# A two-layer diffusion backbone on one core: openings in a fixed order, modulation sums behind them, three direct chunks and another order of transfers in the first sub-layer, norms by chunk

## The chip, the cores and the metric

The kernel runs on one core of a Trainium2 chip. The metric is the device time of one execution in microseconds (us): the time before is the median of three runs. A profile is one further execution, recorded instruction by instruction; its own time is given beside its span (first to last instruction).

## The reference, cut to what matters

Two layers of three sub-layers each, over 512 latent tokens (`x`) and 256 context tokens (`ctx`) of width 1024. All numbers are float32.

```python
def norm_modulate(x, g, shift, scale):
    return rms_norm(x, g) * (1 + scale) + shift

def swiglu(h, w_in, w_out):
    gate, up = jnp.split(h @ w_in, 2, axis=-1)
    return (jax.nn.silu(gate) * up) @ w_out
...
for i in range(DEPTH):                       # DEPTH = 2
    m_lat = (silu(c) @ ada_w[i] + ada_b[i])  # 9 vectors of 1024: shift, scale, gate of 3 sub-layers
    m_ctx = (silu(c_ctx) @ ada_w[i] + ada_b[i])
    x = x + 0.5 * gate * swiglu(norm_modulate(x, ...), ffn_w_in[i, 0], ffn_w_out[i, 0])     # d_ff = 2816
    x = x + gate * mixer(norm_modulate(x, ...))   # layer 0: short gated conv; layer 1: attention, 8 heads, 2 kv heads
    x = x + 0.5 * gate * swiglu(norm_modulate(x, ...), ffn_w_in[i, 1], ffn_w_out[i, 1])
return rms_norm(x_lat, final_g)
```

Every sub-layer runs on both token groups with their own modulation (`m_lat`, `m_ctx`), but for the last one, which runs on the latent tokens alone.

## The kernel before, in words

**Layout and precision.** The stream `x` stays on the chip as eight tiles (m = 0 to 7) of 128 features by 768 tokens. Tokens are cut in two ways: into the two halves of 384 (`TOKENS`, `one` and `two`), or into 512 latent and 256 context tokens (`BOTH`). Each operand of a matmul is split in a rounded part and a rest (`split`: ScalarE copies to the high part, L178, VectorE subtracts for the low part, L179), and each product is three matmuls (`mm3`, L737 to L739).

**Weights.** They come as 512 KB transfers into a ring of five raw buffers (`raw_fill`, L197, SP's queue), are split into eight granules `w` (`w_fill`), and used in the order of one list. The splits of the last `out` of a sub-layer may go into "held" slots that the inputs no longer need.

**A sub-layer (FFN or conv).** Its columns are cut in chunks of two units of 128 columns (gate and up). A chunk is done either *directly*: two token halves times two halves of the features, which is 4 x 4 x 2 x 3 = 96 matmuls of 384 tokens; or by seven *products* of a Strassen-like scheme (M1 to M7; 7 x 4 x 3 = 84 matmuls). A direct step `(c, "01")` is chunk c, token half 0, feature half 1. The products need sums of the inputs (T1 to T4) and their splits, which direct chunks need not, so the first chunks of a sub-layer are direct (`FFN_DIRECT` = 2, `CONV_DIRECT` = 3) while VectorE makes the sums. Part by part of the columns, an `out` phase multiplies by the second weights and adds into `x` (L804, or L861 in the last phase, `out_close`).

**Between sub-layers: the opening.** `out_close` makes a first pass over token half one and a second over half two. Behind each of its matmul groups stand pieces of the next norm: `squares` (L543, L546, L547), `parts` (L566, L567), `root` (the matmul that sums over features, L573 and L574, then the reciprocal root, L555 to L559), `normed` (x times the root, L676), `modulated` (L684) and `parted` (the split into tiles B11, B21 for half one, B12, B22 for half two; 11 and 21 are the two feature halves). The rest stands in hooks behind quarters of the direct steps (`OPENING`): hook `(n, k)` runs after quarter k of step n, hook `n` after step n. Ahead of attention and of the last sub-layer, `out_steps` and `norm_mod` do the same with whole 128-feature chunks and 512, 256 or 128 tokens.

**Modulation.** The first six half-vectors are made by small matmuls during the boot (`ada_direct`, L437 to L445). The other 30 are made in the background by VectorE: `ada_task` has eight steps of sums (`acc`, L454 and L456, one or two per 256 KB transfer `aw`, which POOL issues, L465, two buffers), then `cut` into three bf16 pieces (L486, L488) and `fin`, twelve small matmuls (L494). `bg` runs one step per product from the second chunk behind the direct ones on, and `bg_end` what is left.

**Who sets the order.** TensorE and SP run in the order of the program throughout. ScalarE and VectorE run in the order of a planner, which works from estimated times, but for stretches that are written to keep the program's order (`in_order` to `free_order`): the instructions made in such a stretch keep their order among themselves, and others may be put between them. `keep_in_program_order` ties a single instruction into that order.

Of the kernel before, what the change touches and what calls it, by code (L numbers as in the profile page):

```python
# [36 lines left out]
FFN_DIRECT, CONV_DIRECT = 2, 3  # L37
# [27 lines left out]
HELD_AFTER_T = ((6, 7), (10, 11))  # L65
# [13 lines left out]
def product_order(count, parts, direct, boot=False):  # L79
# [15 lines left out]
    if boot:  # L95
        order += [(0, "00"), (1, "00"), (0, "01"), (1, "01")]
    else:
        order += [(0, "00"), (0, "01"), (1, "00"), (1, "01")]
    for c in range(2):
        order += [(c, "10"), (c, "11")]  # L100
        done(c)
    for c in range(2, direct):
        order += [(c, "10"), (c, "00"), (c, "11"), (c, "01")]
        done(c)
    order += [(direct, m) for m in ("M1", "M2", "M5", "M6")]
# [12 lines left out]
def backbone(ctx: ExitStack, tc: tile.TileContext, a: dict, out: bass.AP):  # L118
# [73 lines left out]
    def raw_fill(most=RAWS):  # L192
        while raw_state["open"] < most and raw_state["loaded"] < len(raws):
            n = raw_state["loaded"]
            src, (u, k), users = raws[n]
            t = wp.tile([P, D], F32, name=f"raw{n}", tag="raw", bufs=RAWS)[:, : u * k * P]
            nc.sync.dma_start(t.rearrange("p (u k c) -> p u k c", u=u, c=P) if len(src.shape) == 4 else t.rearrange("p (k c) -> p k c", c=P), src)  # L197
            raw_tiles[n] = [t.rearrange("p (u k c) -> p u k c", u=u, c=P), users]
            raw_state["loaded"] += 1
            raw_state["open"] += 1  # L200

    def raw_used(n):
        raw_tiles[n][1] -= 1
        if not raw_tiles[n][1]:
            raw_tiles.pop(n)
            raw_state["open"] -= 1

    traced = set()
    held_tiles = {}
    ready = []  # L210
    state = {"next": 0, "open": 0, "extra": 0, "used": 0}

    def place(n, where, k):
# [3 lines left out]
        elif where[0] == "slot":  # L217
            t = slot(where[1], [2, D // 2], f"w{n}")
        else:
# [62 lines left out]
    def add_out(w, k0, npart, held=None, key="", events=(None, None), extra=None, event=None):  # L282
        for m in range(0, KC, 2):
            n = raw_add(w[:, m : m + 2, k0 : k0 + npart, :], (2, npart), 2)
            for u in range(2):
                mm = m + u
                if held and mm < 6:
# [5 lines left out]
    def add_products(key, sources, order, parts, direct, out_w, held):  # L293
# [10 lines left out]
        for c, m in order:  # L304
            if m == "out":
                last = c == len(parts) - 1
                outs = out_w(c)
                add_out(*outs, held=held if last else None, key=f"{key}held", events=((key, "M5"), (key, "M6")))
                continue
            for which in range(2):  # L310
                need(c, which)
            if c >= direct:
                add_product(raw[c, 0], raw[c, 1], m)
            elif (c, m[1]) not in seen:
                seen.add((c, m[1]))
                k0 = 4 * int(m[1])
                for which in range(2):
                    add_plain(raw[c, which], 0, slice(k0, k0 + 4))
# [32 lines left out]
    ffn_order = {boot: product_order(FC, FFN_PARTS, FFN_DIRECT, boot) for boot in (False, True)}  # L351
# [10 lines left out]

    def w_list():
        f0 = starts(LAST_PARTS)

        def ffn_products(i, s):
            b = 2 * i + s // 2
            sources = [[a["ffn_w_in"][b, f][:, z] for z in range(2)] for f in range(FC)]
            f0 = starts(FFN_PARTS)
            add_products(f"f{i}{s}", sources, ffn_order[(i, s) == (0, 0)], FFN_PARTS, FFN_DIRECT, lambda p: (a["ffn_w_out"][b], f0[p], FFN_PARTS[p]), HELD_AFTER_T)  # L370

        ffn_products(0, 0)
# [51 lines left out]
    def ada_load(i, hm, tiles):  # L424
        loaded = []
        for k in range(KC):
            w = tiles[k // 3][:, k % 3, :]
            nc.sync.dma_start(w, a["ada_w"][i, hm, :, k, :])
            loaded.append(w)
        return loaded  # L430

    def ada_direct(i, hm, loaded, tag):

        ps = ptile(tag)
        for k in range(KC):
            g = 32 * (k % 4)
            pe.matmul(ps[g : g + 32, :], boot_tiles["silu"][:, k, :], loaded[k], start=(k < 4), stop=(k >= 4), tile_position=(0, g), skip_group_check=True)  # L437
# [5 lines left out]
        pt = ptile("S", (P, 4, P))  # L443
# [8 lines left out]
    def ada_add(acc, w, k, v, first):  # L452
        if first:
            dve.tensor_scalar_mul(acc, w, silu_c[:, k, v : v + 1])  # L454
        else:
            dve.scalar_tensor_tensor(out=acc, in0=w, scalar=silu_c[:, k, v : v + 1], in1=acc, op0=ALU.mult, op1=ALU.add)  # L456
# [3 lines left out]
    def ada_next(n):  # L460

        if n < len(ada_chunks):
            i, hm, k = ada_chunks[n]
            w = ada_loaded[n] = apool.tile([P, 512], F32, name=f"aw{i}_{hm}_{k}", tag="aw", bufs=2)
            nc.gpsimd.dma_start(w, a["ada_w"][i, hm, :, k, :])  # L465

    def ada_task(i, hm, nv):
# [5 lines left out]
        def step(k):  # L473
# [3 lines left out]
            for v in range(nv):  # L477
                ada_add(st["acc"][:, v, :], w, k, v, k == 0)
# [11 lines left out]
        def fin(v):  # L490
# [5 lines left out]
            if v == nv - 1:  # L496
                ada_done.add((i, hm))
                task_done[0] += 1

        steps = [lambda k=k: step(k) for k in range(KC - 1)]  # L500
        steps.append(lambda: (step(KC - 1), cut(0)))
        if nv == 2:
            steps.append(lambda: (fin(0), cut(1)))
# [1129 lines left out]
```

## Time and profile before

| | |
|---|---|
| median of 3 runs | 2640.86 us (2633.59 to 2642.06) |
| the profiled execution | 2634.72 us, span 2633.0 us, mean granted clock 0.972 |
| TensorE (PE) busy | 2488.1 us, 94% |
| VectorE (DVE) busy | 1960.9 us, 74% |
| ScalarE (ACT) busy | 1169.4 us, 44% |
| moved from HBM | 244.97 MB |

In rows by instruction, a row gives the start, the duration, the engine, the line, `out<-in`, the shapes, and in brackets the idle time of the engine before it with what ended it. Rows of waits give the sum, the count and the longest. A matmul's duration is longer than its distance to the next, since matmuls are pipelined: the distance is what counts. The granted clock is the share of TensorE's full clock that was given.

### The profile page before, as it was taken

What the parts mean: (1) busy time and instruction counts of PE and PEld (TensorE: products, weight loads), DVE (VectorE), ACT (ScalarE), POOL (GpSimd) and SP (SyncE); (2) the same over time, 40 slices, a digit from 0 to 9 for tenths busy, and PEclk for the clock granted to TensorE, in tenths of its full rate; (3) what the DMA queues carried; (4) which work ended last, traced back from release to release, by engine and by line L of the source; (5) the groups of instructions that cost most, each with busy time, mean ns of one, the idle gap of its engine ahead of it and who ended that gap; (6) DMA issues with size and microseconds to landing.
All of it is one profiled execution on the core that took longest, in us unless ns stands there. A gap on an engine that the chain in (4) does not pass through costs nothing.

```text
span 2633.0 us, 36845 instructions
## 1 busy us (share of the span) xinstructions
PE 2488.1 (94%) x14180; PEld 2292.0 (87%) x14180; DVE 1960.9 (74%) x3511; ACT 1169.4 (44%) x2161; POOL 130.9 (5%) x248
## 2 busy tenths in 40 slices
PE   6899999998999899999999899999998999999997
PEld 3799899997989789998999798899997789888886
DVE  5899897568998799888866886766676887644444
ACT  5454353345434544534535453443344785432232
POOL 0010110000000001011000111100000000000000
PEclk9899999998999899999999899999999999999999
DMA  8142342121223123333311243411230201222220
GB/s 321 61 148 96 127 136 74 64 97 59 96 92 95 45 94 125 119 113 129 112 57 60 96 142 111 136 65 65 67 126 33 73 1 53 90 98 96 96 88 33
DMA packets 92193, 249.46 MB, mean 95 GB/s; under 512 B 10224, under 2 KB 19568, under 8 KB 92016
## 3 DMA queue, kind: packets, MB, share of 16 engines
q1 hardware_dynamic: 72816, 184.18, 20.7%
q0 software_dynamic: 19200, 62.93, 7.1%
q8 instruction: 111, 1.82, 0.3%
q14 instruction: 66, 0.54, 0.1%
HBM read 244.97 MB, written 2.10 MB: 94 GB/s over the span
## 4 chain that ended last, share of the span: by engine, by line
PE 59%; issue 21%; DVE 10%; DMA 6%; ACT 3%; POOL 0%; DVEq 0%; POOLq 0%; ACTq 0%
PE ps_A L738 12%; PE ps_A L737 12%; PE ps_A L739 12%; DMA aw<-in_ada_w 6%; PE ps_C L737 5%; PE ps_C L738 5%; PE ps_C L739 5%; DVE acc L456 2%; PE ps_B L737 2%; PE ps_B L738 2%; PE ps_B L739 2%; DVE w L179 1%; PE ps_T L1365 1%; ACT f L684 1%; ACT w L178 0%
## 5 line engine op out<-in xcount | busy, mean ns | idle before, releaser
L178 ACT ACTIVATE w<-raw 128x512 fp32r<-128x512 f32 (+2 forms) x819 | 502.1, 619 | 740.7 <-PE ps_A L739 419.5
L179 DVE TENSOR_TENSOR w<-raw,w 128x512 fp32r<-128x512 f32 (+2 forms) x819 | 550.3, 678 | 194.3 <-ACT w L178 185.6
L456 DVE SCALAR_TENSOR_TENSOR acc<-aw,silu_c,acc 128x512 f32<-128x512 f32 x364 | 266.6, 747 | 59.5 <-DMA aw<-in_ada_w 58.8
L737 PE MATMUL ps_A<-gh,w 128*128 128x512 f32 (+2 forms) x648 | 221.2, 341 | 3.7 <-ACT w L178 3.6
L739 PE MATMUL ps_A<-gh,w 128*128 128x512 f32 (+2 forms) x648 | 221.1, 341 | 1.7 <-DVE w L179 1.7
L738 PE MATMUL ps_A<-gl,w 128*128 128x512 f32 (+2 forms) x648 | 221.2, 341 | 0.5 <-DVE gl L179 0.5
L465 POOL DMA_DIRECT2D aw<-in_ada_w x240 | 129.7, 540 | 1564.3 <-DVE acc L454 895.6
L737 PE MATMUL ps_C<-gh,w 128*128 128x512 f32 (+2 forms) x496 | 177.8, 358 | 19.3 <-DVE g L989 14.0
L804 DVE SCALAR_TENSOR_TENSOR x<-ps_A,gat,x 128x512 f32<-128x512 f32 (+1 forms) x200 | 122.4, 615 | 88.4 <-PE ps_A L739 87.9
L739 PE MATMUL ps_C<-gh,w 128*128 128x512 f32 (+2 forms) x496 | 176.2, 355 | 3.3 <-DVE w L179 3.3
L738 PE MATMUL ps_C<-gl,w 128*128 128x512 f32 (+2 forms) x496 | 177.4, 358 | 0.5 <-DVE gl L179 0.2
L737 PE MATMUL ps_A<-h,w 128*128 128x512 f32 (+1 forms) x424 | 165.3, 390 | 9.3 <-ACT sq L546 9.3
L738 PE MATMUL ps_A<-hl,w 128*128 128x512 f32 (+1 forms) x424 | 165.0, 389 | 0.0
L739 PE MATMUL ps_A<-h,w 128*128 128x512 f32 (+1 forms) x424 | 164.9, 389 | 0.0
L325 DVE TENSOR_TENSOR raw<-raw,raw 128x512 f32<-128x512 f32 x207 | 142.2, 688 | 5.4 <-DMA raw<-in_ffn_w_in 2.8
L737 PEld LDWEIGHTS ps_A<-gh,w 128*128 128x128 f32 x648 | 124.2, 192 | 20.0 <-ACT w L178 4.4
L738 PEld LDWEIGHTS ps_A<-gl,w 128*128 128x128 f32 x648 | 124.0, 191 | 16.2 <-DVE gl L179 1.9
L739 PEld LDWEIGHTS ps_A<-gh,w 128*128 128x128 f32 x648 | 124.1, 192 | 15.5 <-DVE w L179 2.6
L804 DVE SCALAR_TENSOR_TENSOR x<-ps_C,gat,x 128x512 f32<-128x512 f32 (+1 forms) x136 | 87.8, 646 | 54.6 <-PE ps_C L739 54.5
L486 ACT ACTIVATE pc<-acc 128x512 bf16<-128x512 f32 x156 | 95.9, 625 | 71.5 <-DVE acc L488 40.0
L737 PEld LDWEIGHTS ps_C<-gh,w 128*128 128x128 f32 x496 | 95.7, 193 | 34.6 <-issue 15.1
L739 PEld LDWEIGHTS ps_C<-gh,w 128*128 128x128 f32 x496 | 95.7, 193 | 17.0 <-DVE w L179 5.1
(379 smaller groups left out, 6574.7 us busy)
## 6 DMA issues: line engine op xcount, KB each, us to landing
raw<-in_ffn_w_in SPq DMA_DIRECT2D x176, 512.0 KB, 3.7
aw<-in_ada_w POOLq DMA_DIRECT2D x240, 256.0 KB, 3.0
raw<-in_ffn_w_out SPq DMA_DIRECT2D x76, 512.0 KB, 3.9
raw<-in_conv_w_in SPq DMA_DIRECT2D x24, 512.0 KB, 4.1
ada<-in_ada_w SPq DMA_DIRECT2D x37, 256.0 KB, 5.4
raw<-in_attn_w_qkv SPq DMA_DIRECT2D x12, 512.0 KB, 5.2
raw<-in_conv_w_out SPq DMA_DIRECT2D x8, 512.0 KB, 3.6
raw<-in_attn_w_o SPq DMA_DIRECT2D x8, 512.0 KB, 3.6
```

Of the source, the lines that this page charges most:

```text
L178: act.activation(dsth, src, AF.Copy)
L179: dve.tensor_tensor(out=dstl, in0=src, in1=dsth.bitcast(F32), op=ALU.subtract)
L325: dve.tensor_tensor(out=quad(o), in0=quad(x), in1=quad(y), op=ALU.subtract)
L456: dve.scalar_tensor_tensor(out=acc, in0=w, scalar=silu_c[:, k, v : v + 1], in1=acc, op0=ALU.mult, op1=ALU.add)
L465: nc.gpsimd.dma_start(w, a["ada_w"][i, hm, :, k, :])
L486: act.activation(pc, acc, AF.Copy)
L684: act.activation(at, at, AF.Identity, scale=scl[:, m, v : v + 1], bias=mods[i][:, 3 * s, m, v : v + 1])
L737: pe.matmul(ps, wh, xh, start=first, stop=False, **kw)
L738: pe.matmul(ps, wh, xl, start=False, stop=False, **kw)
L739: pe.matmul(ps, wl, xh, start=False, stop=last, **kw)
L804: dve.scalar_tensor_tensor(out=x, in0=p[:, o - off : o - off + w], scalar=gat[:, m, v : v + 1], in1=x, op0=ALU.mult, op1=ALU.add)
L1365: pe.transpose(pt[:, c, :], pr[:, (c0 + c) * P : (c0 + c + 1) * P], ident)
```

## The change

In words:

1. First sub-layer: three direct chunks instead of two, all first token halves ahead of all second ones. The first two weights come as half transfers with the rest behind the shift's weights; the gates' modulation weights go through the ring of raw buffers, the first two background transfers onto SP's queue behind the last direct step. Some splits go to other homes in memory.
2. All openings: the squares, norms and splits stand in a new order, all in program order on ScalarE and VectorE; `modulated` may put every second chunk, or its short pieces, on VectorE. Evictions of direct steps are held and run at a later hook; the fourth pair of banks is B and S.
3. The first two products of the first chunk behind the direct ones (M1, M2) stand ahead of the first `out` phase. A third pair of held slots.
4. Background: the first sum of each sub-layer is tied to the program order, the steps are spread evenly from the eighth product to the last but two chunks, and an empty step (`rest`) stands between `cut` and `fin`.
5. Ahead of attention and of the last sub-layer, the norm is cut in steps of one chunk, put behind groups of the second pass (`PASS_STEPS`); the root of the second group stands later; the last sub-layer opens with three chunks of its first half instead of two.

The diff, cut to its core:

```diff
-FFN_DIRECT, CONV_DIRECT = 2, 3
+FFN_DIRECT, CONV_DIRECT, BOOT_DIRECT = 2, 3, 3
-HELD_AFTER_T = ((6, 7), (10, 11))
+HELD_AFTER_T = ((6, 7), (10, 11), (8, 9))
...
     if boot:
-        order += [(0, "00"), (1, "00"), (0, "01"), (1, "01")]
+        order += [(c, "0" + k) for k in "01" for c in range(direct)]
+        order += [(c, "1" + k) for c in range(direct) for k in "01"]
...
-    order += [(direct, m) for m in ("M1", "M2", "M5", "M6")]
+    order += [(direct, m) for m in ("M1", "M2")]
+    for c in range(direct):
+        done(c)
+    order += [(direct, m) for m in ("M5", "M6")]
...
+            if split:
+                nc.sync.dma_start(dst[:, :, : k // 2], src[:, :, : k // 2])
+                raw_late.append((dst[:, :, k // 2 :], src[:, :, k // 2 :]))
...
+            for hm in (4, 5):
+                boot_raws[hm] = [raw_add(a["ada_w"][0, hm, :, k : k + 2, :].rearrange("p k (j c) -> p k j c", c=P), (2, 4), 2) for k in range(0, KC, 2)]
...
+                ins = ada_add(st["acc"][:, v, :], w, k, v, k == 0)
+                if pinned[0]:
+                    tc.keep_in_program_order(ins)
+            pinned[0] = False
...
         steps.append(lambda: (step(KC - 1), cut(0)))
+        steps.append(rest)
...
+        pace["n"] += 1
+        if pace["n"] < pace["first"]:
+            return
+        span = pace["last"] - pace["first"] + 1
+        due = min(pace["steps"], -(-pace["steps"] * (pace["n"] - pace["first"] + 1) // span))
+        while pace["done"] < due:
+            ada_tasks.pop(0)[1]()
+            pace["done"] += 1
...
-            with tc.manual_schedule(engines=CHAIN_ORDERED):
-                parts = norm_parts(passes[0])
-                run(passes[1], *held[0], False)
-                if width == 2:
-                    run(passes[1], *held[1], False)
-                for step in after(passes[0], parts):
-                    step()
-                for m in range(held[4 - width][0][0]):
-                    sq_add(m, passes[1])
+            in_order()
+            steps = iter(after(passes[0], norm_parts(passes[0])))
+    PASS_STEPS = {1: {0: [("squares", (0,))], 1: [("squares", (1,))], 2: [("norm", 1)], 3: [], 4: [("squares", (2,)), ("norm", 1)], 5: [("norm", 1)], 6: [],
+                      7: [("norm", 7), ("squares", range(3, 8))]},
...
-        behind = {1: [("root", 0)], 2: [("whole", 0, 0, 0)], 3: [("whole", 0, 0, 1), ("parted", 0, 0, 0)], 4: [("whole", 1, 0, 0), ("parted", 0, 0, 1)],
-                  5: [("whole", 1, 0, 1), ("parted", 1, 0, 0)], 6: [("parted", 1, 0, 1), ("squares", 1, range(2))], 7: [("squares", 1, range(2, 6))]}
+        behind = {0: [("squares", 1, [0])], 1: [("root", 0), ("squares", 1, [1]), ("normed", 0, 0, 0)], 2: [("modulated", 0, 0, 0), ("normed", 0, 0, 1), ("parted", 0, 0, 0, "hi"), ("squares", 1, [2])],
...
-    OPENING = {(0, 0): [("squares", 1, range(6, 8)), ("parts", 1)], (1, 1): [("root", 1)], (1, 3): [("whole", 0, 1, 0), ("whole", 0, 1, 1)],
+    OPENING = {(0, 0): [("squares", 1, [7])], (0, 2): [("parts", 1)], (2, 0): [("root", 1)],
+               (2, 1): [("normed", 0, 1, 0), ("modulated", 0, 1, 0, "short"), ("parted", 0, 1, 0, "hi"), ("normed", 0, 1, 1)],
...
+               (3, 1): [("parted", 1, 1, 1, "lo")], (4, 1): [("evict",)], (4, 2): [("sums", "T1", 0)], (4, 3): [("sums", "T1", 1)], (5, 0): [("sum_parted", "T1", 0)],
...
-                if k == 2:
+                if k == 2 and half:
                     w_fill(1)
...
-            scale0 = ada_direct(0, 2, ada_load(0, 2, ada_slots(6, 7, 8)), "C")
-            raw_fill(2)
-            shift0 = ada_direct(0, 0, ada_load(0, 0, ada_slots(9, 10, 11)), "C")
+            scale0 = ada_direct(0, 2, ada_load(0, 2, ada_slots(6, 7, 8)), "C", "A")
+            raw_fill(2, True)
+            shift0 = ada_direct(0, 0, ada_load(0, 0, ada_slots(9, 10, 11)), "C", "A")
+            raw_rest()
+            raw_fill(4)
...
-            gate0 = ada_direct(0, 4, ada_load(0, 4, ada_gs(0, 2) + ada_slots(6)), "B")
-            gate1 = ada_direct(0, 5, ada_load(0, 5, ada_slots(7, 8, 9)), "A")
+            gate0 = ada_direct(0, 4, ada_raws(4), "B")
+            gate1 = ada_direct(0, 5, ada_raws(5), "B")
...
+                     (2, 3): do(("squares", 1, range(4))), (3, 0): do(("squares", 1, range(4, 6)), ("fill", 2)), (3, 1): do(("squares", 1, range(6, 8))), (3, 2): do(("parts", 1), ("fill", 2)),
+                     (4, 0): do(("gate0", 3)), (4, 1): do(("root", 1)), (4, 2): do(("normed", 0, 1, 0), ("modulated", 0, 1, 0, "short"), ("parted", 0, 1, 0, "hi"), ("normed", 0, 1, 1)),
...
+                     (8, 2): do(("gate1", 1)), (8, 3): do(("gate1", 2)), (9, 0): do(("gate0", 1)), (9, 1): do(("gate1", 1)), (10, 1): do(("sums", "T3", 0), ("sums", "T3", 1)),
+                     11: do(("sum_parted", "T1", 0), ("sum_parted", "T1", 1), ("sums", "T2", 0), ("sums", "T2", 1), ("more",)),
...
-            for c in range(2):
-                ps = banks(other, 2)
+            for c in range(3):
+                ps = banks(other, 2)
...
             k_project(lat, 0)
+            q_project(0, 0)
             settle()
-            q_project(0, 0)
```

More of the change, by code (lines that the diff above doesn't have):

```diff
@@ L919, in gated, with products @@
         return got
[L921 removed]
+    behind_outs = []
+    def products(gp, key, order, parts, direct, chunk, straight, out_args, after, passes, hooks, hold):
         live = {}
```

328 lines of the change are left out of this document (189 added, 139 removed).

## The prediction

> **What bounds the kernel now.** I read the page first (shares of the engines), then the stretches of the span, then TensorE's waits, then the order of time where the waits are long.
>
> ```profile
> span 2633.0 us, 36845 instructions
> ...
> PE 2488.1 (94%) x14180; PEld 2292.0 (87%) x14180; DVE 1960.9 (74%) x3511; ACT 1169.4 (44%) x2161; POOL 130.9 (5%) x248
> ```
>
> TensorE (PE) is the bound, and only 145 us of its span are idle. So a change of order alone can win those 145 us and what a slow clock costs beside them, and nothing more. The stretches say where they lie (length, then busy time of each engine, granted clock near the end):
>
> ```profile
> 28.60:60.50 31.90, 28.30 (x170) 20.90 (x170) 18.91 (x36) 15.83 (x29) 1.08 (x2) 0.95 0.93 335
> 60.50:105.50 45.00, 27.60 (x127) 24.96 (x124) 37.89 (x62) 27.19 (x52) 3.24 (x6) 0.75 0.21 71
> 105.50:585.00 479.50, 471.59 (x2839) 451.18 (x2838) 392.16 (x675) 209.36 (x383) 34.51 (x64) 0.99 0.31 105
> 585.00:660.00 75.00, 64.33 (x335) 61.58 (x334) 61.22 (x108) 37.66 (x67) 4.31 (x8) 0.91 0.17 57
> 868.00:940.00 72.00, 55.20 (x254) 48.49 (x253) 58.38 (x92) 40.43 (x75) 4.31 (x8) 0.86 0.19 64
> 940.00:1430.00 490.00, 482.45 (x2925) 461.53 (x2924) 410.61 (x715) 216.08 (x394) 38.84 (x72) 0.99 0.31 105
> 1430.00:1500.00 70.00, 53.10 (x247) 46.98 (x246) 53.20 (x84) 38.58 (x71) 7.01 (x13) 0.88 0.22 75
> 1500.00:1975.00 475.00, 463.01 (x2674) 440.44 (x2673) 337.58 (x566) 190.04 (x352) 26.42 (x49) 0.98 0.30 101
> 1975.00:2030.00 55.00, 45.70 (x237) 39.10 (x237) 36.08 (x71) 22.60 (x42) 0.50 (x2) 0.91 0.06 20
> 2240.00:2262.00 22.00, 17.85 (x122) 17.02 (x120) 18.32 (x46) 12.02 (x30) 0.00 (x0) 0.84 0.18 61
> ```
>
> Length less busy time: 3.6 and 17.4 us idle in the first sub-layer's opening; 10.7, 16.8 and 16.9 us in the three later openings (around 600, 900 and 1460); 7.9, 7.6 and 12.0 us in three long product stretches; 9.3 us before attention; 4.2 us before the last sub-layer. TensorE's waits name what ended the idle time:
>
> ```profile
> PE ps_S L573 <- ACT th L566: 25.1, 6, 5.9
> PE ps_A L737 <- ACT tB12h L178: 23.7, 5, 12.6
> PE ps_C L737 <- DVE g L989: 14.0, 5, 6.2
> PE ps_S L494 <- ACT pc L486: 13.6, 12, 1.5
> ```
>
> The first row is the root's matmul, standing in TensorE's order ahead of matmuls that could run; the second is the second token half (tB12), not yet normed. Each gap costs more than itself: after the longest one the matmuls start 0.32 us apart, and 0.175 us apart once the clock is back.
>
> ```profile
> 73.14 0.69 PE L737 MATMUL ps_A<-tB12h,w 128*128 128x384 f32 x1 [12.58 <-ACT tB12h L178]
> 74.86 0.69 PE L738 MATMUL ps_A<-tB12l,w 128*128 128x384 f32 x1 [1.04 <-DVE tB12l L179]
> 75.34 0.52 PE L739 MATMUL ps_A<-tB12h,w 128*128 128x384 f32 x1
> 75.67 0.52 PE L737 MATMUL ps_C<-tB12h,w 128*128 128x384 f32 x1
> ...
> 80.21 0.34 PE L737 MATMUL ps_C<-tB12h,w 128*128 128x384 f32 x1
> 80.38 0.34 PE L738 MATMUL ps_C<-tB12l,w 128*128 128x384 f32 x1
> ```
>
> From 75.34 to 80.21 that wastes 4.9 x (1 - 0.175/0.32) = 2.2 us; I count 2 us per gap.
>
> Why was tB12 late? VectorE (DVE) runs in order, and sums of the modulation (acc, L456), which nobody needs for hundreds of us, were placed between the steps of the norm:
>
> ```profile
> L456 DVE SCALAR_TENSOR_TENSOR acc<-aw,silu_c,acc 128x512 f32<-128x512 f32 x11 | 7.8, 747 | 2.7 <-DMA aw<-in_ada_w 2.7
> L676 DVE TENSOR_TENSOR f<-x,r 128x768 f32<-128x768 f32 x2 | 1.9, 951 | 0.0
> ```
>
> Between 60.5 and 74.5 these rows are eleven sums, 7.8 us, and 2.7 us of waiting for their transfers, against 1.9 us for two of the norm's own steps.
>
> **The change part by part.**
>
> **1. First sub-layer.** Start: 0.5 MB less of weights (second halves are fetched later) and 0.5 MB less of aw (L465; its first two loads leave POOL's queue for SP's, behind the last direct step) lie ahead of the shift's weights. At some 335 GB/s (the first row above) that is 3 us; the mixed modulation (one of two on VectorE) I give nothing. The first product starts at
>
> ```profile
> 28.61 0.53 PE L737 MATMUL ps_A<-tB11h,w 128*128 128x384 f32 x1 [2.69 <-ACT tB11h L178]
> ```
>
> and can come 0 to 3 us earlier; I take -3, since the DMA share was 0.93 after it and the wait is the end of that chain. A third direct chunk is 96 matmuls instead of 84 (8 products of 12 against 7): 12 x 0.175 = +2.1 us. Its first half (48 matmuls, 8.4 us) stands ahead of tB12, and the eleven sums with their waits (10.5 us) go: 18.9 us of cover against 13.6 us of gap (12.58 + 1.04), so the gap and its cold clock go, -15.6. M1 and M2 (4.2 us) now stand ahead of the first out phase, which today waits twice, and those waits and their cold start go, -5.8 (2.26 + 1.52 + 2):
>
> ```profile
> 98.41 0.49 PE L739 MATMUL ps_C<-gh,w 128*128 128x512 f32 x1 [1.52 <-DVE w L179]
> 101.16 0.80 PE L737 MATMUL ps_C<-gh,w 128*128 128x512 f32 x1 [2.26 <-ACT gh L178]
> ...
> 102.78 0.63 PE L737 MATMUL ps_A<-gh,w 128*128 128x512 f32 x1
> 103.20 0.63 PE L738 MATMUL ps_A<-gl,w 128*128 128x512 f32 x1
> ...
> 109.07 0.40 PE L737 MATMUL ps_C<-gh,w 128*128 128x512 f32 x1
> 109.31 0.39 PE L738 MATMUL ps_C<-gl,w 128*128 128x512 f32 x1
> ```
>
> What it adds: the gate's weights now go through the ring of five raw buffers. Two of gate 0's transfers can be issued only when the pinned splits at step (3,0) have read raw 2 and 3, behind six squares' sums on VectorE. Gate 0's matmuls stand at (4,0) in TensorE's order, and behind them the root and all the rest. One transfer takes 3.7 us:
>
> ```profile
> raw<-in_ffn_w_in SPq DMA_DIRECT2D x176, 512.0 KB, 3.7
> ```
>
> So between 0 (it is hidden) and 3.7 us for it, if the splits end when TensorE arrives; twice that if both come one after the other. By my count the splits end within 1 us of TensorE's arrival, so I take +3.5. Evictions held behind the second half are hidden: pairs go to three banks of A and C, the fourth to B and S. Sum of part 1: -3 + 2.1 - 15.6 - 5.8 + 3.5 = -19, between 0 and -26.
>
> The rows bear on one rule of the skill: after two stalls of 1.52 and 2.26 us, neither above 2.3, the 512-wide matmuls were 0.42 us apart until 105 and 0.23 apart at 109. The Trainium skill (TensorE: Matmul & The Clock Gate, Part 1) says that the clock is halved after an idle window of about 3.4 us, so that shorter stalls would cost only themselves; the trace does not agree, and the sum goes by the trace. By that rule the forecast would be about 2 us lower for this out phase's kind of stall in each of the two later ones that I leave standing, some 4 us in all.
>
> **2. The three later openings.** Idle 44.4 us. The squares now go with the second pass, one per step, so that one sum instead of six or so is left behind its last x (five of some 0.5 us, by the 256-wide one of part 4), and the root stands 18 matmuls later (after the first quarter of the third direct step, not half of the second), 3.2 us: some 5.7 to 6 us against a wait of 5.9. That just does, and I count all three root waits gone, -17.7. TB12's other waits, 23.7 - 12.6 = 11.1 us, go as in part 1, since the sums are pinned behind it. Waits for weights at the first out phase (some 4 us in two openings) half go by M1 and M2 and by the third held pair of slots, -4. Of about eight cold starts six go, -12. What is late next is VectorE itself, now in fixed order. From the second pass to M5, 72 us of TensorE, it holds two token halves of norm (about 20 + 11 us), the sums and splits of T1 to T4 (16 x 0.95 = 15), evictions (4), weights (8) and x (10): an estimate of 69 us from counts in the code and from the rows above, with 0.48 us for a 256-wide x (row in part 4). That is nearly full, so I give back 1 us each: -17.7 - 11.1 - 4 - 12 + 3 = -42, between -20 (the roots and one cold start each go, nothing else) and -58.
>
> **3. Pace of the modulation sums.** A rest step stands between cut and fin, so that TensorE no longer stands behind pc: -13.6. In the sub-layer from 1500 one step per product becomes 80 steps over 118 products, so a sum has 3.1 us instead of 2.1; today VectorE waits there for aw, and TensorE for it (L989, 14.0 us).
>
> ```profile
> 64.90 1.42 DVE L456 SCALAR_TENSOR_TENSOR acc<-aw,silu_c,acc 128x512 f32<-128x512 f32 x2 [1.93 <-DMA aw<-in_ada_w]
> ```
>
> That is -11 with two cold starts of 2. In the first and third FFN the pace hardly falls (108 steps on 111 products, 120 on 118), and the sums now reach into stretches that have none today. I take half of 28: -14, between 0 and -27.
>
> **4. Norm by chunk ahead of attention.** There TensorE waited 9.3 us, until the last eviction of x had been made, behind all eight norms on VectorE:
>
> ```profile
> 2006.43 0.74 DVE L616 SCALAR_TENSOR_TENSOR hl<-t,mods,h 128x512 fp32r<-128x512 f32 x1
> ...
> 2007.43 0.48 DVE L804 SCALAR_TENSOR_TENSOR x<-ps_A,gat,x 128x256 f32<-128x256 f32 x1
> ```
>
> Now only two norms stand ahead of them. Each further chunk costs VectorE 1.5 us and TensorE 1.4, so the rest keeps step: -9.3 - 2 + 2 = -9, between -4 and -11. Before the last sub-layer the third chunk (some 6 us) covers the root's 3.5: -4, between 0 and -6.
>
> **Sum.** -19 - 42 - 14 - 9 - 4 = -88. The profiled execution took 2634.72 us (span 2633.0 and 1.7 around it), 6 below the median of the runs, 2640.86; 2634.7 - 88 = 2547.
>
> **Rivals.**
> *The pinned order stalls on transfers.* In the first sub-layer ScalarE and VectorE may not pass a split whose raw weights are on the way, and gate 0 waits for both transfers. Then part 1 gives nothing: 2547 + 19 = 2566. For it: the 1.93 us row above, where everything behind a sum stood still. Against it: the DMA share falls to 0.21 after 60.5. Of the queues the Trainium skill (TensorE: Matmul & The Clock Gate, section on the array's architecture) says that VectorE and ScalarE are strictly first in, first out; the trace agrees with that 1.93 us.
> *VectorE becomes the bound of the openings.* 69 of 72 us is my estimate; 10% more makes 4 us per opening and its cold start, and pacing gives half: 42 falls to 24 and 14 to 7: 2572. For it: VectorE was busy 37.9 of 45 us. Against: the sums leave.
> *The pin does not hold.* Only the first sum of each sub-layer is pinned. If others slip ahead, parts 1 and 2 lose their tB12 terms (15.6 + 11.1): 2574. Against it: later sums follow the first through its accumulator.
> *Slower: weights starve.* The direct steps of a first half no longer start a split; only later steps do. If each of the ten quads after an opening (M1, M2, eight of out) waited for its transfer and split, 3.7 + 1.3 = 5 us less its own 2.1 us of matmuls, that is 2.9 x 10 x 4 = 116 us, so 2547 + 116 = 2663. It decides from 88 / 40 = 2.2 us per quad on. Against it: the weights needed first are split before the opening, and SP loads as soon as a buffer frees.
>
> **How the numbers follow.** Forecast 0.66, first rival 0.10, second 0.10, third 0.05, slower 0.06, no change that can be told 0.03. About 0.3% (8 us) is what a measurement of this kernel can tell from no change. All parts at their high ends give 2634.7 - 128 = 2507, at their low ends (0 - 20 - 0 - 4 - 0) 2611. I take 2515 to 2600, which leaves out some 2 in 10. The likeliest alone is 2520 to 2570.
>
> **What would show it.** Right: the root waits and tB12 fall below 5 us in sum; no acc row on VectorE before the first out phase; the four stretches of openings have a clock above 0.95; pc and the 9.3 us are gone; TensorE idles some 70 us less. Wrong: TensorE waiting for ada or raw transfers around 50 us, for w after the openings, or VectorE above 95% in them.

## The result, and the profile after

The changed kernel takes 2568.13 us (median of four runs, 2567.70 to 2570.03) against 2638.61 us in the runs beside it: a ratio of 0.9736, with a 95% interval of 0.9717 to 0.9754. It is faster by about 70 us, where 88 were forecast. The profiled execution took 2568.54 us, span 2566.8 us at a mean granted clock of 0.983. The page of the profile after:

```profile
span 2566.8 us, 36910 instructions
...
PE 2467.6 (96%) x14240; PEld 2284.7 (89%) x14240; DVE 1955.4 (76%) x3539; ACT 1152.2 (45%) x2121; POOL 129.4 (5%) x246
```

Of the 66.2 us between the two spans, 46 are idle time of TensorE (145 to 99 us) and 20 its busy time: nearly the same matmuls at a better clock. TensorE's waits after, with their sum, count and longest, show two new names, gd and x (pc are the bf16 pieces of the modulation's sums; g and gd are a chunk's outputs on their way out of the banks, gd those of a direct chunk):

```profile
PE ps_S L531 <- ACT pc L523: 21.2, 12, 4.1
PE ps_C L803 <- DVE g L1076: 13.5, 7, 6.2
...
PE ps_B L803 <- ACT gd L1137: 5.6, 2, 2.8
...
PE ps_A L803 <- DVE x L870: 5.0, 2, 4.0
```

The roots (25.1 us before) and tB12 (23.7) are gone from the top. The pieces of the modulation sums, pc, rose from 13.6 to 21.2 us, and g stayed (14.0 before). To see where the time went, I cut both spans at the same two points of the work: at the first matmul of a sub-layer's last out phase, and at its first M5 (the first matmul with T1). The stretches, length, TensorE's busy time, granted clock and DMA, before:

```profile
0.00:123.00 123.00, 86.17 (x436) 0.89 0.55 198
123.00:568.20 445.20, 437.29 (x2643) 0.99 0.33 111
568.20:673.90 105.70, 95.03 (x509) 0.94 0.13 45
673.90:841.00 167.10, 165.70 (x998) 1.00 0.34 109
841.00:957.10 116.10, 99.30 (x511) 0.91 0.13 46
957.10:1402.50 445.40, 437.85 (x2666) 0.99 0.34 114
1402.50:1519.50 117.00, 100.10 (x510) 0.91 0.17 57
1519.50:1964.30 444.80, 432.81 (x2521) 0.98 0.30 101
```

and after:

```profile
0.00:131.10 131.10, 103.23 (x533) 0.93 0.54 178
131.10:557.30 426.20, 419.87 (x2558) 1.00 0.36 115
557.30:646.90 89.60, 89.60 (x510) 1.00 0.13 42
646.90:821.40 174.50, 167.94 (x997) 0.98 0.36 112
821.40:916.70 95.30, 92.51 (x511) 0.96 0.12 39
916.70:1370.20 453.50, 438.19 (x2666) 0.98 0.36 115
1370.20:1464.60 94.40, 91.51 (x510) 0.98 0.13 40
1464.60:1908.00 443.40, 432.21 (x2522) 0.99 0.35 110
```

Odd rows are openings, even rows are the product stretches behind them. (The first two of after hold one direct chunk more and one product chunk less: 14.7 us of products, 84 x 0.175, are to be taken from the first and added to the second when they are compared.) That gives the ledger; the last two rows come from the same cuts in attention and in the last sub-layer:

| part | forecast | trace |
|---|---|---|
| first sub-layer up to M5 | -19 | -6.6 |
| the three later openings | -42 | -16.1 - 20.8 - 22.6 = -59.5 |
| product stretches (pace of the sums) | -14 | -4.3 + 7.4 + 8.1 - 1.4 = +9.8 |
| up to the end of attention | -9 | -10.3 |
| last sub-layer | -4 | +0.4 |
| sum | -88 | -66.2 |

So the sum came out near partly by luck, by errors that cancel in part: the openings gave 17 us more, the first sub-layer 12 and the pacing 24 less.

### The profile page after: what moved, and what is told of

Its sections match the earlier page's. It is cut to its first block, busy times and chain, and to the rows that moved or that the text cites. A ratio compares the mean times of both kernels' runs of the same rounds, so it can differ in the third digit from the quotient of the medians.

```text
span 2566.8 us, 36910 instructions
## 1 busy us (share of the span) xinstructions
PE 2467.6 (96%) x14240; PEld 2284.7 (89%) x14240; DVE 1955.4 (76%) x3539; ACT 1152.2 (45%) x2121; POOL 129.4 (5%) x246
## 4 chain that ended last, share of the span: by engine, by line
PE 55%; issue 26%; DVE 8%; DMA 8%; ACT 2%; SPq 1%; POOL 0%; DVEq 0%; POOLq 0%; ACTq 0%
PE ps_A L804 11%; PE ps_A L803 11%; PE ps_A L805 11%; DMA aw<-in_ada_w 7%; PE ps_C L803 4%; PE ps_C L804 4%; PE ps_C L805 4%; DVE acc L490 2%; PE ps_B L803 2%; PE ps_B L804 2%; PE ps_B L805 2%; DVE w L179 1%; PE ps_T L1464 1%; DMA raw<-in_ffn_w_in 1%; DVE raw L346 0%
## 5 line engine op out<-in xcount | busy, mean ns | idle before, releaser
L178 ACT ACTIVATE w<-raw 128x512 fp32r<-128x512 f32 (+2 forms) x810 | 493.3, 619 | 699.3 <-PE ps_A L805 383.5
L179 DVE TENSOR_TENSOR w<-raw,w 128x512 fp32r<-128x512 f32 (+2 forms) x810 | 542.0, 677 | 177.5 <-ACT w L178 170.9
L490 DVE SCALAR_TENSOR_TENSOR acc<-aw,silu_c,acc 128x512 f32<-128x512 f32 x364 | 266.5, 747 | 66.7 <-DMA aw<-in_ada_w 65.8
L803 PE MATMUL ps_A<-gh,w 128*128 128x512 f32 (+1 forms) x624 | 213.1, 342 | 4.2 <-DVE x L870 4.0
L804 PE MATMUL ps_A<-gl,w 128*128 128x512 f32 (+1 forms) x624 | 213.1, 341 | 0.4 <-DVE gl L179 0.4
L805 PE MATMUL ps_A<-gh,w 128*128 128x512 f32 (+1 forms) x624 | 212.1, 340 | 0.0
L803 PE MATMUL ps_C<-gh,w 128*128 128x512 f32 (+1 forms) x472 | 167.6, 355 | 13.5 <-DVE g L1076 13.5
L804 PE MATMUL ps_C<-gl,w 128*128 128x512 f32 (+1 forms) x472 | 167.3, 354 | 0.4 <-DVE gl L179 0.4
L805 PE MATMUL ps_C<-gh,w 128*128 128x512 f32 (+1 forms) x472 | 166.8, 353 | 0.0
L803 PEld LDWEIGHTS ps_A<-gh,w 128*128 128x128 f32 x624 | 119.3, 191 | 20.0 <-DVE x L870 4.5
L804 PEld LDWEIGHTS ps_A<-gl,w 128*128 128x128 f32 x624 | 119.3, 191 | 16.1 <-DVE gl L179 1.9
L805 PEld LDWEIGHTS ps_A<-gh,w 128*128 128x128 f32 x624 | 119.2, 191 | 13.0
L803 PEld LDWEIGHTS ps_C<-gh,w 128*128 128x128 f32 x472 | 90.5, 192 | 27.3 <-issue 13.4
L803 PE MATMUL ps_A<-tB11h,w 128*128 128x384 f32 x312 | 107.1, 343 | 3.6 <-ACT tB11h L758 3.6
```

Of the source, the lines that this page charges most:

```text
L178: act.activation(dsth, src, AF.Copy)
L179: dve.tensor_tensor(out=dstl, in0=src, in1=dsth.bitcast(F32), op=ALU.subtract)
L490: return dve.scalar_tensor_tensor(out=acc, in0=w, scalar=silu_c[:, k, v : v + 1], in1=acc, op0=ALU.mult, op1=ALU.add)
L803: pe.matmul(ps, wh, xh, start=first, stop=False, **kw)
L804: pe.matmul(ps, wh, xl, start=False, stop=False, **kw)
L805: pe.matmul(ps, wl, xh, start=False, stop=last, **kw)
```

## The experiments

Ratios are against the kernel before on the same chip (its medians there were 2631.7 to 2638.6 us); the changed kernel has 0.9736. The pin is the tie of a sub-layer's first modulation sum to the program's order.

| run | edit to the changed kernel | median us | ratio [95%] |
|---|---|---|---|
| e1 | halves along k | 2559.44 | 0.9724 [0.9710, 0.9739] |
| e2 | *before*, with the pin | 2678.94 | 1.0179 [1.0163, 1.0194] |
| e3 | no pin | 2545.32 | 0.9671 [0.9654, 0.9687] |
| e4 | steps paced over out phases too | 2537.55 | 0.9639 [0.9625, 0.9654] |
| e5 | no pin, pace of before | 2548.02 | 0.9670 [0.9655, 0.9686] |
| e6 | no pin, no rest steps | 2560.90 | 0.9719 [0.9701, 0.9737] |
| e7 | e1 + e4 + other banks | 2534.65 | 0.9619 [0.9602, 0.9636] |
| e8 | e7 without the pin | 2536.26 | 0.9619 [0.9600, 0.9638] |
| e9 | four aw buffers | 2549.59 | 0.9687 [0.9672, 0.9701] |
| e10 | e7 + later T3, T4 | 2527.20 | 0.9600 [0.9585, 0.9614] |
| e11 | e10 + four aw buffers | 2515.53 | 0.9555 [0.9539, 0.9571] |
| e12 | e11 + a second rest | 2510.20 | 0.9540 [0.9524, 0.9556] |

**e1: where the late start came from.** The changed kernel's first product came at 33.48 us, not earlier than the 28.61 of before. ScalarE's and TensorE's rows of after:

```profile
25.93 0.63 ACT L178 ACTIVATE w<-raw 128x512 fp32r<-128x512 f32 x1 [7.95 <-DMA raw<-in_ffn_w_in]
27.56 0.63 ACT L178 ACTIVATE w<-raw 128x512 fp32r<-128x512 f32 x1 [0.99 <-DMA raw<-in_ffn_w_in]
28.09 0.58 ACT L476 ACTIVATE adr<-ps_C 128x512 f32<-128x512 f32 x1
...
33.48 0.69 PE L803 MATMUL ps_A<-tB11h,w 128*128 128x384 f32 x1 [3.64 <-ACT tB11h L758]
```

ScalarE stands 8 us in fixed order at a split of the first weight; the shift's row copy (adr) stands behind it, and all products behind that. The DMA rows of the first 34 us explain it: the two early transfers carry 16 KB each and the two late ones 496 KB. These weights have three axes, `(p k c)`, so the cut at `[:, :, : k // 2]` takes 4 of 128 columns.

```diff
-nc.sync.dma_start(dst[:, :, : k // 2], src[:, :, : k // 2])
+nc.sync.dma_start(dst[:, : k // 2], src[:, : k // 2])     # and the rest, [:, k // 2 :], likewise
```

> The changed kernel with one edit: the two early raw weights are cut in halves along k, not along the 128 columns. In the changed kernel the cut takes 4 of 128 columns (16 KB each), and 496 KB of each stand behind the shift's weights in SP's queue; ScalarE stands in fixed order at the first split (7.95 us idle for raw) and the shift's row copy stands behind it. Theory: that is why the first product started at 33.48 us and not near 28.6; with real halves it starts at 26 to 29 us, nothing later moves against it, and the time is 2560 to 2564 against 2568.1. Rival: the bytes ahead of the shift's weights set the start (now 512 KB instead of 32 KB ahead of them, some 1.4 us at 347 GB/s); then the first product stays between 32 and 35 us and the time between 2566 and 2570.

```profile
27.64 0.69 PE L803 MATMUL ps_A<-tB11h,w 128*128 128x384 f32 x1 [2.67 <-ACT tB11h L758]
```

In e1 (the row above) the first product comes 5.8 us earlier, and the last out phase of the sub-layer starts 5.3 us earlier (552.0 against 557.3 us). Not all of it is ScalarE's stand: the shift's last matmuls ended at 25.15 us in the changed kernel and at 23.63 in e1, so some 1.5 of the 5.8 us went with the transfers themselves. The place is shown. The gain over the whole run is not: the intervals of the ratios overlap.

**e2 and e3: what the pin does.** My prediction had the pin as the cure of the late tB12. e2 adds it alone to the kernel before:

```diff
-ada_add(st["acc"][:, v, :], w, k, v, k == 0)
+ins = ada_add(st["acc"][:, v, :], w, k, v, k == 0)
+if pinned[0]:                      # set for the first sum of each sub-layer
+    tc.keep_in_program_order(ins)
```

> The kernel before with one edit: the first sum of each sub-layer's modulation is pinned to its place in program order, as in the changed kernel; nothing else. Theory A (of the prediction): the sums on VectorE made tB12 late, so the waits for tB12 (23.7 us, 5 times) fall below 10 us, no sum stands on VectorE between 60 and 74 us, and the time is 2615 to 2628 against 2638.6. Rival B: the root's place and the squares set when tB12 is ready and the sums only fill VectorE's idle time; then tB12's waits stay above 18 us and the time within 4 us of 2638.6. Rival C: the openings gain as in A but the displaced sums come back as waits in the product stretches, and the time is 2630 to 2638.

No theory named this time: it is 46 us *slower*. By the cuts of the stage table the openings are shorter (3.7 us in the first, 2.1 + 2.8 + 3.2 in the later ones) and the four product stretches longer, by 18.3 + 18.4 + 17.1 + 0.6 = 54.4 us: theory C in kind, and far beyond its size. TensorE's waits of e2:

```profile
PE ps_S L497 <- ACT pc L489: 51.0, 33, 3.1
...
PE ps_A L741 <- ACT tB12h L178: 17.7, 6, 10.6
```

No sum stands on VectorE between 60 and 75 us any more, and yet the wait for tB12 fell only from 12.6 to 10.6 us. The sums made it late by some 2 us and no more. ScalarE's rows of the kernel before point to what did the rest:

```profile
60.15 3.61 ACT L684 ACTIVATE f<-f,mods,scl 128x128 f32<-128x128 f32 x8 [4.14 <-DVE f L676]
63.78 1.28 ACT L1050 ACT_TABLE_LOAD   x1
65.08 0.49 ACT L1050 ACTIVATE gd<-ps_A 128x384 f32<-128x384 f32 x1
...
68.90 0.58 ACT L441 ACTIVATE adr<-ps_B 128x512 f32<-128x512 f32 x1
70.49 1.86 ACT L684 ACTIVATE f<-f,mods,scl 128x128 f32<-128x128 f32 x4 [1.01 <-DVE f L676]
72.26 0.82 ACT L178 ACTIVATE tB12h<-f 128x768 fp32r<-128x768 f32 x1
```

Twelve short modulations of 0.45 us, and between them the eviction of two pairs with its table load, its Silu steps and splits, and a row copy: from 63.78 to 69.5 us ScalarE does work that tB12 does not need, and VectorE, in the same fixed order, makes the second normed piece only behind it, at 69.50. The changed kernel holds those evictions for a later hook and gives the short pieces to VectorE, which my prediction had costed at nothing. (The Trainium skill, ScalarE: Activation LUTs, What ACT_TABLE_LOAD costs, gives 1.28 us for the load and 1.38 us for a drain beside it; the 1.28 agrees, and with 0.02 us to the row ahead of it and to the row behind it no drain is seen here.) That this order alone cures tB12 was not tried by itself. The changed kernel's rows say how the gap closed:

```profile
72.37 0.85 ACT L758 ACTIVATE tB12h<-f 128x768 fp32r<-128x768 f32 x1
74.27 0.44 PE L804 MATMUL ps_B<-tB12l,w 128*128 128x384 f32 x1 [0.51 <-DVE tB12l L760]
```

By the time of the span tB12h is ready no earlier than before (73.22 against 73.08 us). Counted from the first product it is 4.7 us earlier (39.7 against 44.5): from the root's th (53.10 before, 64.99 after) to tB12h the chain takes 8.2 us instead of 20.0, but it begins later. The other 8 us are cover: TensorE now has 48 more matmuls ahead of tB12, the first half of the third direct chunk, which the prediction had counted at 8.4. What the pin costs is seen from the other side in e3, the changed kernel without it:

```diff
-pinned[0] = True
+pinned[0] = False
```

> The changed kernel without the pin on the first sum of each sub-layer; the new order of the openings stays. Theory A: the pin keeps the sums out of the openings; without it they slip ahead of the second token half's norm again, tB12's waits come back in part (up to the 15.6 and 11.1 us that the prediction gave them), and the time is 2578 to 2595. Rival B: the fixed order of the openings keeps them out by itself and the time is within 3 us of 2568.1. Rival C: the sums fill idle time of VectorE in the openings at no cost there and free the product stretches, which lost 7.4 and 8.1 us in the changed kernel; then it is 2553 to 2563.

It is faster by 0.0065 of 2639 us, that is 17 us by the ratios and 24 by the spans, and went further than rival C. Its rows for pc and tB12:

```profile
PE ps_A L804 <- DVE tB12l L760: 4.7, 4, 1.5
...
PE ps_S L531 <- ACT pc L523: 1.6, 2, 1.4
```

By the same cuts, the openings lose 4.9 + 3.4 + 2.7 + 3.5 = 14.5 us without the pin and the product stretches gain 6.9 + 8.6 + 16.3 + 5.9 = 37.7. Against the kernel before, the three later openings are still 12.7 + 18.1 + 19.1 = 49.9 us shorter: most of their 59.5 us comes from the rest of the change and not from the pin. A free planner runs the sums ahead of their place in the program, and TensorE's `fin` finds its pieces ready. With the pin the whole train of sums starts late and stays late.

**e4 and e5: the pace.** Three rows of VectorE and one of TensorE, in the changed kernel:

```profile
948.99 1.41 DVE L490 SCALAR_TENSOR_TENSOR acc<-aw,silu_c,acc 128x512 f32<-128x512 f32 x2
950.33 0.68 DVE L346 TENSOR_TENSOR raw<-raw,raw 128x512 f32<-128x512 f32 x1
950.93 0.68 DVE L525 TENSOR_TENSOR acc<-acc,pc 128x512 f32<-128x512 f32 x1
...
950.46 0.19 PE L531 MATMUL ps_S<-ones_b,pc 128*128 128x1 bf16 x1 [4.07 <-ACT pc L523]
```

VectorE works without a gap, in order: sums, weight differences, then the subtraction that the next piece needs, while TensorE stands at `fin`, two steps behind the last sum. e4 spreads the same steps over the out phases too, where VectorE has room:

```diff
 for grp in groups:                 # an out phase
     run(grp, ms, units, major)
+    for _ in ms:
+        bg(1)                      # one unit of weight per column block, as much as a product
...
-due = min(pace["steps"], -(-pace["steps"] * (pace["n"] - pace["first"] + 1) // span))
+due = min(pace["steps"], -(-pace["steps"] * pace["w"] // pace["weight"]))
```

> The changed kernel with the modulation's steps paced over the out phases too (one unit of weight per product, one per out column block and token group; the same first and last product). Theory A: per chunk of seven products (14.7 us of TensorE) VectorE has some 10.6 us of work of its own, and seven steps with 1.4 us sums make it 18 us, so the sums make evictions and the pieces of pc late; an out column block leaves VectorE some 2.3 us of 4.2 free. With the steps spread, pc waits (21.2 us) and the waits for g (13.5) fall by half or more, and the time is 2538 to 2555. Rival B: these waits come from the chain acc, pc, acc, pc itself, whatever the load; then pc and g waits stay within 5 us of their sums and the time within 4 us of 2568.1. Rival C: the sums collide with the evictions of x in the out phases, new waits on x or w there take the place of the old ones, and the time is 2566 to 2580.

```profile
PE ps_S L531 <- ACT pc L523: 5.8, 4, 2.1
```

Theory A, with that row: pc falls from 21.2 to 5.8 us and the stretches by 4.7, 3.1, 17.5 and 6.1 us, while the openings lose 2.0 us in the first and under 1 us in the others. g did not fall by half (13.5 to 9.8). e5 asks whether the new pace is worth anything without the pin:

```diff
-bg()                               # steps spread evenly from the eighth product on
+if direct < c < total - 2: bg()    # one step per product
+elif c == total - 2 and m == "M1": bg_end()
```

> The changed kernel without the pin (2545.3 us) and with the pace of the kernel before as well: one step of the modulation per product from the chunk behind the direct ones, what is left at once two chunks before the end; the rest steps stay. Theory A: the sums run ahead of their program place by themselves, so the new pace is worth nothing; 2542 to 2549, and the product stretch of the last of these sub-layers (437.5 us without the pin) stays within 2 us. Rival B (the prediction's): slowing one step per product to 80 on 118 is what took the waits for g in that stretch; then it goes back to 441 to 446 us and the time to 2549 to 2556.

Nothing: the ratio is that of e3, and the last product stretch is 438.3 us against 437.5. The prediction's -11 for it falls, as far as a run without the pin can tell.

**e6: the rests.** Both `steps.append(rest)` go, from e3.

> The changed kernel without the pin (2545.3 us) and without the rest steps between cut and fin. Theory A: a rest takes away the wait for pc as the prediction said, and only the pin hid it; without rests pc waits come back from 1.6 us to 10 to 16 us and the time is 2553 to 2565. Rival B: it was the lead of the sums that took the pc waits, and rests are worth nothing; pc stays below 5 us and the time within 4 us of 2545.

Without the pin, rests are worth 0.0048 of 2639, that is 12.7 us, as theory A had it; but pc came back to 6.3 us only, not to 10 or more. So 4.7 of the 12.7 are pc waits; the others are waits for a second `fin` behind the first one's result (2.5 us), for c, and the clock behind them.

**e9: why g is late.** VectorE waits in order for a transfer, and TensorE for VectorE, in the changed kernel:

```profile
1529.19 0.75 DVE L490 SCALAR_TENSOR_TENSOR acc<-aw,silu_c,acc 128x512 f32<-128x512 f32 x1 [4.08 <-DMA aw<-in_ada_w]
...
1536.08 0.77 PE L803 MATMUL ps_C<-gh,w 128*128 128x512 f32 x1 [6.15 <-DVE g L1076]
```

```diff
-tag="aw", bufs=2)                  # ada_next(n0 + k + 2)
+tag="aw", bufs=2), and tag="aw2", bufs=2 for every other two   # ada_next(n0 + k + 4)
```

> The changed kernel, pin kept, with four aw buffers instead of two in the last two of the sub-layers that carry modulation sums (the two added ones lie where the convolution's tiles were). An aw transfer lands 3.8 us after its issue, and today two sums close together leave VectorE waiting in order for the third (4.08 us at 1529). Theory A: these waits are what makes g late for TensorE; its waits for g in the stretch behind 1465 us (10.7 us, longest 6.2) fall below 3 us, VectorE's waits for aw (65.8 us in all) by half, pc stays, and the time is 2552 to 2561 against 2568.1. Rival B: VectorE is late by its own work there; g waits stay above 8 us and the time within 4 us of 2568.1. Rival C: without the waits the sums bunch more and pc or x gets later: 2566 to 2574.

```profile
PE ps_C L813 <- DVE g L1086: 3.0, 3, 2.2
```

That row of e9 stands against 13.5 us, 7 waits. VectorE's own waits for aw fell from 65.8 to 21.4 us, and the last two stretches by 7.1 and 12.1 us. (The 3.8 us of the expectation is the median of e7 between 1480 and 1516 us; over the whole changed kernel it is 3.1.) Too few aw buffers made g late, more than the pace did: e4's spread alone had left 9.8 of the 13.5 us.

**e7, e8 and e10: out phases that wait for x.** In the changed kernel's first out phase VectorE makes the last of T3 and T4 ahead of the first evictions of x:

```profile
111.95 0.95 DVE L179 TENSOR_TENSOR tT4l<-fT,tT4h 128x768 fp32r<-128x768 f32 x1
112.82 1.82 DVE L179 TENSOR_TENSOR tT3l<-fT,tT3h 128x768 fp32r<-128x768 f32 x2
...
115.76 0.74 DVE L870 SCALAR_TENSOR_TENSOR x<-ps_C,gat,x 128x512 f32<-128x512 f32 x1
...
117.22 0.58 PE L803 MATMUL ps_A<-gh,w 128*128 128x256 f32 x1 [4.04 <-DVE x L870]
```

In the two later openings of this kind the wait stood one place earlier, at M2's bank (gd, 2.8 us each). e7 puts e1 and e4 together and gives the third pair the banks B and S; e8 is e7 without the pin.

```diff
-ptile(t, (P, NH)) for t in ("BS" if pairs[0] == 3 else "AC")
+ptile(t, (P, NH)) for t in ("BS" if pairs[0] == 2 else "AC")   # 3 in the first sub-layer
```

> The changed kernel, pin kept, with three edits: raw halves along k (e1, which gained 4 us against its own before), sums paced over the out phases too (e4: 2537.6), and the third pair of banks instead of the fourth on B and S, so that M2 does not find its bank taken by the pair just ended (M2 waited 2.8 us for gd in two openings, and a cold start behind each). If they add up: 2537.6 - 5 - 2 x (2.8 + 2) = 2522 to 2530. If B is then late for something else (the root's S bank, or the third pair's own eviction), the bank gives nothing: 2530 to 2536.

> The same three edits without the pin. Theory A: with the sums spread over the out phases the product stretches need no lead any more, so the pin only keeps the openings clean; without it the openings lose the 2.7 to 4.9 us each that e3 lost and the stretches gain less: 2528 to 2540, slower than with the pin by 4 to 12. Rival B: the lead that the sums take without the pin is worth as much here (23 us): 2500 to 2515.

The waits for gd went, and as many came for x (5.2 us in e4, 10.5 in e7): the bank gave nothing. With the spread pace the pin makes no difference any more, which neither theory had. e10 records T3 and T4 behind the out phase:

```diff
-12: do(T2 splits, T4 sums, T3 splits), 13: do(T4 splits)     # first sub-layer
+12: do(T2 splits), 15: do(T4 sums, T3 splits), 17: do(T4 splits)
-hooks 8 and 9                                                # later ones: the same pieces
+hooks 11 and 13
```

> e7 (2534.7 us) with the sums and splits of T3 and T4 recorded behind the first out phase instead of ahead of it, in the first sub-layer and the two later ones of that kind. In e7 VectorE makes 6 to 12 us of them ahead of the first evictions of x, and TensorE waits 4.04, 2.74 and 2.72 us for x, with a cold start each. Theory A: these three waits fall below 1 us each and the time is 2518 to 2528. Rival B: VectorE's planner puts the sums first wherever they are recorded, and nothing moves: 2530 to 2537. Rival C: T3 or T4 is then late for its own product and TensorE waits there as long: 2530 to 2540.

```profile
PE ps_A L803 <- DVE x L870: 1.0, 1, 1.0
```

With that row (10.5 us, 4 waits, in e7) theory A holds: the openings are shorter by 9.2, 5.8 and 3.0 us, though the first stretch gives back 5.8. The span is 10.9 us shorter; the intervals of the two ratios just overlap.

**e11 and e12: together.** e11 is e10 with e9's buffers, e12 a second `rest`.

> e10 with e9's four aw buffers. If e9's theory A and e10's theory A both hold and add up: g's 6.4 us wait and its cold start go as well, 2508 to 2520. If the pacing over the out phases has already taken what the buffers give: within 3 us of e10.

> e11 (2515.5 us) with two rest steps instead of one between cut and fin. TensorE still waits 10.9 us, seven times, for pc, always within some 60 us behind an opening, where the pinned sums start late. Theory A: the chain acc, pc, acc, pc, acc, pc needs only a little more time than one step gives it; with a second rest pc falls below 4 us, and the time is 2502 to 2511. Rival B: VectorE's backlog behind the pin grows with the closer steps and pc comes as late as before; pc stays above 8 us and the time is 2512 to 2520.

They add up. The step from e11 to e12 by itself (0.0015) lies within the intervals, but pc went from 10.9 us to 3.5 as theory A said. In e12 g is 3.8 us, and TensorE is busy for 98% of the span:

```profile
span 2509.3 us, 36924 instructions
...
PE 2447.6 (98%) x14240; PEld 2269.6 (90%) x14240; DVE 1948.7 (78%) x3539; ACT 1154.6 (46%) x2121; POOL 129.3 (5%) x246
```

2510.2 us is 4.6% below the kernel before and 2.0% below the changed one (0.9540 / 0.9736).

## Why the prediction was right, and where it was not

The time fell in the range (2515 to 2600) and on the forecast's side, 21 us above 2547. That waits in the openings cost the most, and their cold clock with them, was right; that the sum came this near was in part luck, as the table above shows. Step by step:

1. **Start, -3: wrong, +4.9.** I read "half transfers" from the words of the code and counted 0.5 MB less ahead of the shift; the cut took the wrong axis (with halves along k, in e1, the first product comes at 27.64, 1.0 us earlier than before). The first rival was right in kind here: ScalarE stood in pinned order at a split whose weights were on the way, for 7.95 us. Its second half, gate 0 waiting for its transfers (+3.5), did not come: its matmuls ran at 63.77 without a wait.
2. **First sub-layer's tB12, -15.6: the gap went, to 0.5 us, but only half of the cover was as reckoned.** Of the 18.9 us of cover, the third chunk's 8.4 came. The step that failed is the other 10.5, "sums of the modulation ... were placed between the steps of the norm" as the cause: e2 took away every sum and left 10.6 of the 12.6 us. I showed VectorE's rows and never ScalarE's. What closed the rest is a shorter chain from th to tB12h (8.2 us instead of 20.0), for which the evictions held back and the pieces given to VectorE are the likely reason, not tried alone.
3. **First out phase, -5.8: not gained.** The waits for w and gh went, and 4.04 us for x came at the same place, from T3 and T4 (e10). I had counted only the waits that go, and not what stands ahead of the next work on VectorE once TensorE arrives there earlier.
4. **Later openings, -42: mis-sized, -59.5.** Idle time fell from 44.4 to 5.7 us, more than the 32.8 that I had named, and the slow clock gave 20.8 instead of 12. The 3 us that I gave back to VectorE are the 5.6 us for gd. By e3 the pin's share of the 59.5 is about 10; the other parts were not tried one by one.
5. **Pacing, -14: wrong, +9.8.** Three terms. The rest's -13.6 was near in size (12.7 in e6, without the pin), but only 4.7 of it was the wait for pc that I had named, so the match is partly luck; and with the pin pc rose to 21.2 us. The slower pace in the last of the four, -11, was worth nothing without the pin (e5); g was late for its transfers (e9). And sums that left the openings were paid again in the stretches, which I had mentioned in half a sentence and not costed.
6. **Attention, -9: right, -10.3.** The 9.3 us wait is 1.0. **Last sub-layer, -4: nothing.** The second root's 3.46 us went, and two waits for hl (1.94 and 1.83 us), behind the norms on VectorE, came in its place.

Of the signs that I had named, the later openings' clock (1.00, 0.96, 0.98), the roots, tB12 and the missing acc rows were as forecast; pc, the first opening's clock (0.93), and TensorE's idle time (46 us less, not some 70) were not. The third rival was off the mark: the pin held, and that was its harm. The second, VectorE as the bound of the openings, did not show there but one stretch later. Weights did not starve: no wait for w is left among TensorE's waits.

## What to carry to other kernels

When an operand is late, read the queues of *all* engines on its chain between the last good point and the wait before naming a cause; the sums that fill an engine's idle time looked guilty here and made 2 of the 12.6 us. Background work was better spread by the room of the engine that does it than by a count of steps of another (e4). An order constraint on its first piece was paid by those who wait for its last one, until the spread left room behind it (e3, e8). A stage table with cuts at the same work in both traces shows errors that cancel in the total.

## What was not expected of the hardware

Stalls of one length do not have one effect on the clock. After one of 2.79 us the 384-wide matmuls were 0.32 us apart at once, at a granted clock of 0.50 (changed kernel, the first three rows); after one of the same length at the same place in e1 they stayed 0.175 apart, at 1.00 (the last three):

```profile
894.90 0.69 PE L803 MATMUL ps_B<-tB21h,w 128*128 128x384 f32 x1 [2.79 <-ACT gd L1137]
895.39 0.52 PE L804 MATMUL ps_B<-tB21l,w 128*128 128x384 f32 x1
895.71 0.52 PE L805 MATMUL ps_B<-tB21h,w 128*128 128x384 f32 x1
```

```profile
891.18 0.44 PE L803 MATMUL ps_B<-tB21h,w 128*128 128x384 f32 x1 [2.79 <-ACT gd L1137]
891.46 0.34 PE L804 MATMUL ps_B<-tB21l,w 128*128 128x384 f32 x1
891.63 0.34 PE L805 MATMUL ps_B<-tB21h,w 128*128 128x384 f32 x1
```

So it went with 1.53 us of waiting for tB12l: in e3 (608.72 us) the distance was 0.32 half a microsecond later, in e5 (610.35 us) it stayed 0.175. A stall of 1.5 us can be enough, then, and one of 2.8 us need not be. The Trainium skill (TensorE: Matmul & The Clock Gate, Part 1) puts the change at an idle window of about 3.4 us that runs freely. That equal stalls end differently agrees with a window that runs freely; that stalls of about half that length can bring the change does not agree with the length. A stall that does so costs its cold stretch as well: after a second one of 2.79 us in the changed kernel, the distance was 0.32 us from 1443.79 to 1447.16, which is 3.4 x (1 - 0.175/0.32) = 1.5 us more.
